# Hybrid encoder block in float32 on one core: own PSUM banks for three products, other pauses in two normalisations, first loads of the second MLP matrix on ScalarE's queue

## The chip, the core and the metric

The program runs on one core of a Trainium2 chip. The metric is the device time of one execution in microseconds (us). Five engines take instructions in order, each from a queue of its own: TensorE (PE), VectorE (DVE), ScalarE (ACT), GpSimd (POOL) and SyncE (SP, which here only issues DMAs). Matrix products are accumulated in PSUM. The kernel uses its eight banks as two rings of four tiles each, called `mm` and `aux`.

## The reference, cut

```python
def block(x, c, ...):                        # 1024 prompt rows, and 8 x 16 sample rows
    ...
    h = rms_norm(x, norm_g[0]) * (1 + sc1) + sh1
    m, conv_state, h_fin, v = mixer(h, ...)                    # ends in "@ w_out"
    x = x + g1 * rms_norm(m, norm_g[1])
    h = rms_norm(x, norm_g[2]) * (1 + sc2) + sh2               # second normalisation
    f = jnp.square(jax.nn.relu(h @ w_ff1)) @ w_ff2             # (1152,1024)x(1024,4096), x(4096,1024)
    x = x + g2 * rms_norm(f, norm_g[3])
    return x, conv_state, h_fin.astype(x.dtype), v
```

## The kernel before, in words

The 1152 rows are 9 tiles of 128, in three groups of three: groups 0 and 1 are prompt rows, group 2 is two prompt tiles (6, 7) and the sample tile (8). A float32 product is made of three: each operand is split into a rounded high part and the low rest (`split`: a CAST, L236 on ACT or L238 on DVE, then a subtraction on DVE, L239), and PE computes high·high, high·low and low·high. With four blocks of depth 128 one *product* is 12 matmuls of 128x384 (`prod`, L1359 to L1361).

In time the program is: the mixer; its output projection, of which `m_out(2)` for group 2 comes last; the first MLP matrix (`m_f1`); the second (`m_f2`).

**`m_f1`** goes through 26 *units*, each one pair p of 128-column blocks of w_ff1 for one or more groups. For groups 0 and 1 together most pairs use a Strassen-like scheme with seven products instead of eight: A11, S2, S1, S3, A12, A22, S4. S1 to S4 are sums of weight blocks (L1330), the other operands T1 to T4 are sums of normalised inputs (`t_task`). Kinds of unit: "g0", "g1", "g2" (one group, four products, PSUM tiles W1 and W2 of `aux`), "fast" (the seven products), "full" (fast and g2 of the same pair interleaved, 11 products). Before: units 0 to 2 are g0, 3 to 5 g1, 6 to 9 fast (NH = 4), then 7 g2 and 9 full.

A fast unit takes three tiles X, Y, Z of `mm`. X collects A11 and then A12, Y collects S2, S3 and A22, Z collects S1 and S4. DVE reads them in between: after S2 `u2 = p1 + Y` (L1467), after S3 `u3 = p1 + Y; u3 += Z` (L1476, L1477), after A22 `p1 += Y` (L1490), after S4 `u2 += Z` (L1500). PE may write Y or Z again only when the read before is done. ACT squares the ReLU of each result (L1369, L1370), and SP stores it.

The weights' operands are prepared five products ahead (`f1_prep(at + 5)`): ACT casts, DVE subtracts. From these results DVE forms sums for the second matrix (`f_sums`, L1382 to L1385), which SP stores in `fdS`. `w_sums` does the same for pieces wt0 to wt15 of w_ff2 (L1402 to L1406), which SP stores in `td`.

**The second normalisation** of group g is `prep2_task(g)`. Per tile: ACT sums the squares (`prep_stat`, L420, into a scratch tile "junk" of the one-buffer ring `tb`, which `f_sums` uses for fS1 too); DVE scales (L465; L452 for the first tile); then twice a half (`prep_half`): four PE transposes into a tile pt2*th* (t the tile, h the half), scale and shift (`modulate`: on ACT, four L428, for tiles 0 to 7; on DVE, L434 and L435, for tile 8), and the split into h2T. Tile 3 to 5 is group 1, 6 to 8 group 2. Group 1's transposes stand partly in `m_out(2)`, partly behind units 0 to 2; group 2's stand in the fast units; `w_sums` begins when group 2 is done.

**What sets the order.** No scheduler: the program steps its tasks by a virtual clock as it is written out, and the table WAIT holds their pauses in virtual nanoseconds. A longer pause puts the next step further back in every engine's queue. The engines then run these queues in order, and wait for data.

**Between the two matrices.** The last unit (25) calls `f2_open` after its S1 product: four DMAs on SP, ar0 and ar1 (stored results, batches A11 and Ga) and br0, br1 (w_ff2). ACT and DVE split these into as0, as1, bs0 and so on, the first operands of `m_f2`, whose first three PSUM tiles P00, P01, P02 are the next of `mm`.

Of the kernel before, what the change touches and what calls it, by code (L numbers as in the profile page):

```python
# [14 lines left out]
ALU = mybir.AluOpType  # L15
# [3 lines left out]
P = 128  # L19
# [3 lines left out]
GT = 3  # L23
GW = 384
DFF = 4096
NG = 3
NH = 4
GELU_A = 0.044715
GELU_S = 0.7978845608028654

# [11 lines left out]
def shape_constants():  # L42
# [20 lines left out]
    pn0=1900, pn1=0, pn2=3800, prep1_load=17400, prep1_load1=1700, prep1_load2=3200, prep1_next=13800,  # L63
    prep1_next1=4400, prep1_next2=1000, prep1_norm=11500, prep1_norm1=3300, prep1_norm2=800, prep1_split=40000,
    prep1_split1=400, prep1_split2=1000, prep1_stat=6500, prep1_stat1=1000, prep1_stat2=0, prep1_tr=5600,
    prep1_tr1=0, prep1_tr2=3500, prep2_load=1700, prep2_load0=200, prep2_load1=5200, prep2_load2=3600,
    prep2_next=3200, prep2_next0=1500, prep2_next1=4400, prep2_next2=1500, prep2_norm=6200, prep2_norm0=9900,
    prep2_norm1=7200, prep2_norm2=2600, prep2_split=1700, prep2_split0=800, prep2_split1=800, prep2_split2=0,
    prep2_stat=9600, prep2_stat0=0, prep2_stat1=4400, prep2_stat2=1200, rr=11700, rr0=800, rr1=13000, rr2=400,
    set_load=10000, set_pcc=0, set_pw=2900, sp=13000, sp0=800, sp1=500, sp2=1900, sp_mid=22500, sp_mid0=9600,  # L70
    sp_mid1=0, sp_mid2=1400, sz=20900, sz0=1300, sz1=800, sz2=0, x1=14700, x10=7300, x11=7200, x12=4700, xr=29300,
    xr0=10000, xr1=2600, xr2=2700, yT=45700, yT0=2500, yT1=5600, yT2=2800, yc=23700, yc0=15400, yc1=16900,
# [11 lines left out]
def wait(key, g=""):  # L84
    return float(WAIT.get(f"{key}{g}", WAIT[key]))
# [33 lines left out]
def tile_block(ctx, tc, io, out):  # L119
    nc = tc.nc  # L120
    pe, act, dve, pool, sync = nc.tensor, nc.scalar, nc.vector, nc.gpsimd, nc.sync
    load = sync.dma_start
# [29 lines left out]
    def mmt(name):  # L152
        return ps.tile([P, 512], F32, tag="mm", name=name)

    def auxt(name):
        return ps.tile([P, 512], F32, tag="aux", name=name)
# [77 lines left out]
    def split(hi, lo, src, on_act=False):  # L234
        if on_act:
            act.copy(hi, src)  # L236
        else:
            dve.tensor_copy(hi, src)  # L238
        dve.tensor_tensor(lo, src, hi.bitcast(F32), op=ALU.subtract)  # L239
# [7 lines left out]
    def transpose4(src, name):  # L247
        pt = auxt(name)
        for k in range(4):
            pe.transpose(pt[:, P * k:P * k + P], src[:, P * k:P * k + P], ident)  # L250
        return pt
# [99 lines left out]
    modT = {}  # L351
# [71 lines left out]
    def modulate(h, src, t, which, half):  # L423
        G, sh = modT[f"G{which}"], modT[f"sh{which}"]
        if t < 8:
            for k in range(4):
                kk = 4 * half + k
                act.activation(h[:, k, :], src[:, k, :], AF.Identity, scale=G[:, kk, 0:1], bias=sh[:, kk, 0:1])  # L428
        else:
            v = src.rearrange("p k (s i) -> p k s i", s=8)  # L430
            h4 = h.rearrange("p k (s i) -> p k s i", s=8)
            gb = G[:, 4 * half:4 * half + 4, 1:9].unsqueeze(3).to_broadcast([P, 4, 8, 16])
            sb = sh[:, 4 * half:4 * half + 4, 1:9].unsqueeze(3).to_broadcast([P, 4, 8, 16])
            dve.tensor_tensor(h4, v, gb, op=ALU.mult)  # L434
            dve.tensor_tensor(h4, h4, sb, op=ALU.add)  # L435

    def prep_half(x, t, dst, off, half):
        pt = transpose4(x[:, 512 * half:512 * half + 512], f"pt2{t}{half}")
        h = x[:, 512 * half:512 * half + 512].rearrange("p (k i) -> p k i", k=4)
        modulate(h, pt.rearrange("p (k i) -> p k i", k=4), t, 2, half)  # L440
        yield wait("prep2_split", t // GT) if t < 8 else 300.0
        for k0, n, d in dst[half]:
            split(d[:, :, 0, off:off + P], d[:, :, 1, off:off + P], h[:, k0:k0 + n, :], ENG["p2hi"])
# [796 lines left out]
    p1 = laneB.add(prep1_task(2, ssd_tasks[1]))  # L1240
# [14 lines left out]
    TV = {}  # L1255
# [43 lines left out]
    units = [(p, "g0") for p in range(NG)] + [(p, "g1") for p in range(NG)]  # L1299
    units += [(p, "fast") for p in range(NG, NG + NH)] + [(p, "g2") for p in range(NG + NH)]  # L1300
    units += [(p, "full") for p in range(NG + NH, NU)]
    FULL = ("A11", "S2", "S1", "S3", "A12", "A22", "S4", "A21")
# [46 lines left out]
    def two(name):  # L1349
        t = wp.tile([P, 2, GW], F32, tag="raw", name=name, bufs=2)  # L1350
        return t[:, 0], t[:, 1]
# [4 lines left out]
    def prod(bank, op, xs, first, last):  # L1356
        for k in range(4):
            x = xs[k]
            pe.matmul(bank, op[:, 0, k, :], x[:, 0], start=first and k == 0, stop=False, skip_group_check=True)  # L1359
            pe.matmul(bank, op[:, 0, k, :], x[:, 1], start=False, stop=False, skip_group_check=True)  # L1360
            pe.matmul(bank, op[:, 1, k, :], x[:, 0], start=False, stop=last and k == 3, skip_group_check=True)  # L1361
# [4 lines left out]
    def f_out(n, p, src, q=None):  # L1366

        q = src if q is None else q
        act.activation(q, src, AF.Relu)  # L1369
        act.activation(q, q, AF.Square)  # L1370
        if n != "A21":
            f_save(n, p, q)
# [38 lines left out]
    def m_f1():  # L1411
        at = 0
        for u, (p, kind) in enumerate(units):
# [8 lines left out]
            def take(n):  # L1422
                nonlocal at
                at += 1
                f1_prep(at + 5)
                return ops[u, n]
# [29 lines left out]
            X, Y, Z = [mmt(f"{n}{u}")[:, 0:GW] for n in "XYZ"]  # L1456
            o = take("A11")
            prod(X, o, hk(0, 0), True, True)
            pu = ta.tile([P, 2, GW], F32, tag="x", name=f"pu{u}", bufs=2)
            p1, u2 = pu[:, 0], pu[:, 1]  # L1460
# [10 lines left out]
            if u == len(units) - 1:  # L1471
                f2_open()
            yield 12 * 175.0
            prod(Y, take("S3"), TV[3], False, True)
            u3, a11 = two(f"u3_{u}")
            dve.tensor_tensor(u3, p1, Y, op=ALU.add)  # L1476
            dve.tensor_tensor(u3, u3, Z, op=ALU.add)  # L1477
            f_out("A22", p, u3)
            yield 12 * 175.0
            o = take("A12")  # L1480
# [5 lines left out]
                f_out("Ga", p, W1, qa)  # L1486
            yield 12 * 175.0
            o = take("A22")
            prod(Y, o, TV[4], False, True)
            dve.tensor_tensor(p1, p1, Y, op=ALU.add)  # L1490
            f_out("A12", p, p1)
            if full:
# [26 lines left out]
    ops2, araw, asp, braw = {}, {}, {}, {}  # L1519
    pos2 = dict(job=0, araw=0, braw=0)  # L1520

    def a_load(upto):
        while pos2["araw"] <= min(upto, len(batches) - 1):
            k = pos2["araw"]
            i, q, n = batches[k]
            if k % 4 == 1:
                araw[k] = fp.tile([P, 4, GW], F32, tag="t2", name=f"ar{k}")
            else:
                araw[k] = fslot((2, None, 0, 1)[k % 4], [P, 4, GW], F32, f"ar{k}")
            load(out=araw[k], in_=fd[n][q])  # L1530
            pos2["araw"] += 1

    def b_load(upto):
        while pos2["braw"] <= min(upto, len(jobs2) // 2 - 1):
            r = pos2["braw"]
            i, u = jobs2[2 * r]
            b = PASSES[i][1]
            t = fp.tile([P, KD, P], F32, tag="raw1", name=f"br{r}", bufs=4).rearrange("p (u k) i -> p u (k i)", u=2)
            if b in td:
                finish(ws)  # L1540
                load(out=t, in_=td[b][u // 2])
            else:
                x, c = int(b[1]) - 1, int(b[2]) - 1
                load(out=t, in_=wv[x][:, u:u + 2, 512 * c:512 * c + 512])
            braw[r] = t
            pos2["braw"] += 1

    def f2_open():
        a_load(1)
        b_load(1)  # L1550

    def f2_prep(upto):
        while pos2["job"] < min(upto, len(jobs2)):
# [214 lines left out]
```

## Time and profile before

| | us |
|---|---|
| three executions | 1393.88, 1397.48 (median), 1398.32 |
| the profiled execution, its own time | 1396.9 |
| its span in the profile | 1395.1 |
| busy in the span: PE, DVE, ACT, POOL | 1278.1, 858.7, 609.5, 255.2 |

The span is what the profiler saw between first and last instruction; 1.8 us of the execution lie outside it. PE is busy 92% of the span, but the engines' shares are averages over stages: in the fast units PE waits, and in the full units it doesn't. "Idle before" in a row is the time in which the engine did nothing before that instruction, and the name behind the arrow is what ended it.

### The profile page before, as it was taken

What the parts mean: (1) busy time and instruction counts of PE and PEld (TensorE: products, weight loads), DVE (VectorE), ACT (ScalarE), POOL (GpSimd) and SP (SyncE); (2) the same over time, 40 slices, a digit from 0 to 9 for tenths busy, and PEclk for the clock granted to TensorE, in tenths of its full rate; (3) what the DMA queues carried; (4) which work ended last, traced back from release to release, by engine and by line L of the source; (5) the groups of instructions that cost most, each with busy time, mean ns of one, the idle gap of its engine ahead of it and who ended that gap; (6) DMA issues with size and microseconds to landing.
All of it is one profiled execution on the core that took longest, in us unless ns stands there. A gap on an engine that the chain in (4) does not pass through costs nothing.

```text
span 1395.1 us, 18656 instructions
## 1 busy us (share of the span) xinstructions
PE 1278.1 (92%) x6815; PEld 1132.2 (81%) x6815; DVE 858.7 (62%) x1349; ACT 609.5 (44%) x1131; POOL 255.2 (18%) x275
## 2 busy tenths in 40 slices
PE   6988888898989999789789999999799999999996
PEld 4966867687789967679689999999788888887874
DVE  4667799466676633687675566766553335336766
ACT  3333423344445524765535444444443334344461
POOL 1233574136341443220000000000000000001013
PEclk9999889999999999889999999999999999999998
DMA  8687646735687558656258865656694437345863
GB/s 312 206 283 260 204 143 207 256 136 187 200 314 251 191 204 318 234 176 217 87 175 300 311 235 199 241 213 213 222 369 154 157 134 267 144 155 185 316 242 120
DMA packets 106259, 304.70 MB, mean 218 GB/s; under 512 B 11844, under 2 KB 32324, under 8 KB 106168
## 3 DMA queue, kind: packets, MB, share of 16 engines
q1 hardware_dynamic: 106056, 303.21, 62.0%
q8 instruction: 53, 0.87, 0.3%
q14 instruction: 38, 0.31, 0.1%
q0 software_dynamic: 112, 0.31, 0.1%
HBM read 231.43 MB, written 72.04 MB: 218 GB/s over the span
## 4 chain that ended last, share of the span: by engine, by line
PE 62%; DVE 14%; DMA 11%; ACT 6%; issue 4%; POOL 2%; SPq 1%; DVEq 0%; ACTq 0%; POOLq 0%
PE P L1630 4%; PE P L1631 4%; PE P L1629 4%; PE W L1360 4%; PE W L1361 4%; PE W L1359 4%; PE G L1630 3%; PE G L1629 3%; PE G L1631 3%; DMA kl<-wl 2%; DMA wr<-in_w_a_dram 2%; PE Y L1359 2%; PE Y L1361 1%; PE Y L1360 1%; DMA x<-in_x_prompt_dram 1%
## 5 line engine op out<-in xcount | busy, mean ns | idle before, releaser
L239 DVE TENSOR_TENSOR bs<-br,bs 128x512 fp32r<-128x512 f32 x128 | 93.7, 748 | 124.1 <-ACT bs L236 124.0
L236 ACT CAST bs<-br 128x512 fp32r<-128x512 f32 x128 | 77.7, 618 | 163.7 <-PE G L1631 102.9
L1630 PE MATMUL P<-bs,as 128*128 128x512 f32 x336 | 132.7, 395 | 3.0 <-DVE bs L239 3.0
L1629 PE MATMUL P<-bs,as 128*128 128x512 f32 x336 | 132.8, 395 | 1.0 <-DVE acc L1692 1.0
L1631 PE MATMUL P<-bs,as 128*128 128x512 f32 x336 | 132.6, 395 | 0.0
L243 POOL TENSOR_SCALAR fr<-fss 128x1 f32<-128x1 f32 x9 | 2.8, 316 | 635.0 <-DVE fss L1589 634.9
L239 DVE TENSOR_TENSOR as<-ar,as 128x1536 fp32r<-128x1536 f32 x44 | 81.0, 1845 | 57.9 <-ACT as L236 57.9
L327 POOL TENSOR_TENSOR wl<-wr,wh 128x1024 fp32r<-128x1024 f32 (+1 forms) x28 | 70.0, 2503 | 110.0 <-ACT wh L320 50.1
L236 ACT CAST as<-ar 128x1536 fp32r<-128x1536 f32 x44 | 64.9, 1479 | 48.1 <-PE P L1631 28.3
L1630 PEld LDWEIGHTS P<-bs,as 128*128 128x128 f32 x336 | 63.4, 189 | 18.1 <-DVE bs L239 3.9
L1629 PEld LDWEIGHTS P<-bs,as 128*128 128x128 f32 x336 | 63.5, 189 | 16.5 <-DVE acc L1692 1.9
L315 ACT CAST wh<-wr 128x1024 fp32r<-128x1024 f32 (+1 forms) x44 | 46.1, 1048 | 69.7 <-PE wo L1000 23.0
L1630 PE MATMUL G<-bs,as 128*128 128x512 f32 x192 | 75.4, 393 | 0.0
L1631 PEld LDWEIGHTS P<-bs,as 128*128 128x128 f32 x336 | 63.5, 189 | 14.5
L1629 PE MATMUL G<-bs,as 128*128 128x512 f32 x192 | 75.2, 392 | 0.0
L1631 PE MATMUL G<-bs,as 128*128 128x512 f32 x192 | 75.2, 392 | 0.0
L596 PE MATMUL xbc<-hT,wl 128*128 128x384 f32 x144 | 51.3, 356 | 4.3 <-DMA wl<-kl 4.3
L643 DVE SCALAR_TENSOR_TENSOR cva<-pre,cwh,cva 128x256 f32<-128x256 f32 (+1 forms) x78 | 44.5, 611 | 13.9 <-ACT pre L624 12.1
L594 PE MATMUL xbc<-hT,wh 128*128 128x384 f32 x144 | 52.2, 362 | 0.0
L595 PE MATMUL xbc<-hT,wh 128*128 128x384 f32 x144 | 50.6, 351 | 0.0
L583 PE MATMUL pv<-wh,hT 128*128 128x256 f32 x144 | 43.1, 300 | 3.3 <-DVE vt L566 3.3
L584 PE MATMUL pv<-wl,hT 128*128 128x256 f32 x144 | 41.8, 290 | 4.0 <-POOL wl L327 4.0
(945 smaller groups left out, 3782.3 us busy)
## 6 DMA issues: line engine op xcount, KB each, us to landing
wf<-in_w_f_dram SPq DMA_DIRECT2D x52, 512.0 KB, 5.4
wl<-kl SPq DMA_DIRECT2D x42, 512.0 KB, 4.3
wt<-in_w_ff_dram SPq DMA_DIRECT2D x16, 1024.0 KB, 6.0
td<-wt SPq DMA_DIRECT2D x64, 256.0 KB, 2.6
br<-in_w_ff_dram SPq DMA_DIRECT2D x32, 512.0 KB, 3.9
br<-td SPq DMA_DIRECT2D x32, 512.0 KB, 3.6
kl<-wl SPq DMA_DIRECT2D x26, 512.0 KB, 6.6
wr<-in_w_o_dram SPq DMA_DIRECT2D x24, 512.0 KB, 5.3
```

The source lines that it names most:

```text
L236: act.copy(hi, src)
L239: dve.tensor_tensor(lo, src, hi.bitcast(F32), op=ALU.subtract)
L327: (pool if i in LO_POOL else dve).tensor_tensor(lo, raw, hi.bitcast(F32), op=ALU.subtract)
L594: pe.matmul(out, wh, xh, start=first, stop=False)
L595: pe.matmul(out, wh, xl, start=False, stop=False)
L596: pe.matmul(out, wl, xh, start=False, stop=last)
L1359: pe.matmul(bank, op[:, 0, k, :], x[:, 0], start=first and k == 0, stop=False, skip_group_check=True)
L1360: pe.matmul(bank, op[:, 0, k, :], x[:, 1], start=False, stop=False, skip_group_check=True)
L1361: pe.matmul(bank, op[:, 1, k, :], x[:, 0], start=False, stop=last and k == 3, skip_group_check=True)
L1629: pe.matmul(bank, x[:, 0], b[:, 0], start=first, stop=False, skip_group_check=True)
L1630: pe.matmul(bank, x[:, 0], b[:, 1], start=False, stop=False, skip_group_check=True)
L1631: pe.matmul(bank, x[:, 1], b[:, 0], start=False, stop=last, skip_group_check=True)
```

## The change

Five edits:

1. NH is 5: one pair moves from a full unit to a fast and a g2 unit. There are now 27 units: 3 g0, 3 g1, 5 fast (6 to 10), 8 g2, 8 full. The products are the same in number.
2. In fast and full units S3 has a tile Y7 of its own (`mm`) and A22 a tile Y4 (`aux`): Y, Y7 and Y4 are each written once. `p1 = u2 + Y7; u3 = p1 + Z` replaces the two additions after S3. X and Z are still written twice.
3. Group 1's pauses are shorter, group 2's longer.
4. For second halves of tiles 3, 4, 5 scale and shift are four operations on DVE (new L442) in place of four on ACT.
5. `f2_open` issues its four DMAs on ScalarE's queue.

```diff
-NH = 4
+NH = 5
...
-    prep1_tr1=0, prep1_tr2=3500, prep2_load=1700, prep2_load0=200, prep2_load1=5200, prep2_load2=3600,
-    prep2_next=3200, prep2_next0=1500, prep2_next1=4400, prep2_next2=1500, prep2_norm=6200, prep2_norm0=9900,
-    prep2_norm1=7200, prep2_norm2=2600, prep2_split=1700, prep2_split0=800, prep2_split1=800, prep2_split2=0,
-    prep2_stat=9600, prep2_stat0=0, prep2_stat1=4400, prep2_stat2=1200, rr=11700, rr0=800, rr1=13000, rr2=400,
+    prep1_tr1=0, prep1_tr2=3500, prep2_load=1700, prep2_load0=200, prep2_load1=1500, prep2_load2=3600,
+    prep2_next=3200, prep2_next0=1500, prep2_next1=2500, prep2_next2=5000, prep2_norm=6200, prep2_norm0=9900,
+    prep2_norm1=3500, prep2_norm2=5000, prep2_split=1700, prep2_split0=800, prep2_split1=800, prep2_split2=1500,
+    prep2_stat=9600, prep2_stat0=0, prep2_stat1=2500, prep2_stat2=4500, rr=11700, rr0=800, rr1=13000, rr2=400,
...
-        modulate(h, pt.rearrange("p (k i) -> p k i", k=4), t, 2, half)
+        if half and t // GT == 1:
+            for k in range(4, 8):
+                dve.tensor_scalar(h[:, k - 4, :], pt[:, P * (k - 4):P * (k - 3)], modT["G2"][:, k, 0:1],
+                                  modT["sh2"][:, k, 0:1], op0=ALU.mult, op1=ALU.add)
+        else:
+            modulate(h, pt.rearrange("p (k i) -> p k i", k=4), t, 2, half)
...
-            prod(Y, take("S3"), TV[3], False, True)
+            Y = mmt(f"Y7{u}")[:, 0:GW]
+            prod(Y, take("S3"), TV[3], True, True)
             u3, a11 = two(f"u3_{u}")
-            dve.tensor_tensor(u3, p1, Y, op=ALU.add)
-            dve.tensor_tensor(u3, u3, Z, op=ALU.add)
+            dve.tensor_tensor(p1, u2, Y, op=ALU.add)
+            dve.tensor_tensor(u3, p1, Z, op=ALU.add)
             f_out("A22", p, u3)
...
-            prod(Y, o, TV[4], False, True)
+            Y = auxt(f"Y4{u}")[:, 0:GW]
+            prod(Y, o, TV[4], True, True)
             dve.tensor_tensor(p1, p1, Y, op=ALU.add)
...
-    def a_load(upto):
+    def a_load(upto, load=load):
...
-    def b_load(upto):
+    def b_load(upto, load=load):
...
     def f2_open():
-        a_load(1)
-        b_load(1)
+        a_load(1, act.dma_start)
+        b_load(1, act.dma_start)
```

How this moves instructions is shown at three places (the first matmul of a group stands for it; names carry the tile and the unit).

**PE, end of `m_out(2)` and the first units.** pt2*th* are transposes, wo21x matmuls of `m_out(2)`, W10 and W20 the first unit's products. Before:

```order
L250 MATMUL pt231_5347<-cs_81,M1_4566 128x128 x4
...
L250 MATMUL pt220_5368<-cs_81,A0_4956 128x128 x4
...
L250 MATMUL pt221_5414<-cs_81,A0_4956 128x128 x4
L250 MATMUL pt240_5425<-cs_81,M1_4566 128x128 x4
L1359 MATMUL W10_5434<-h2T00_5055,op0A11_5388 128x384
...
L250 MATMUL pt241_5555<-cs_81,M1_4566 128x128 x4
...
L250 MATMUL pt250_5655<-cs_81,M1_4566 128x128 x4
...
L250 MATMUL pt251_5750<-cs_81,M1_4566 128x128 x4
L1359 MATMUL W13_5779<-h2T100_5052,op3A11_5632 128x384
```

Now:

```order
L250 MATMUL pt240_5299<-cs_81,M1_4566 128x128 x4
...
L250 MATMUL pt211_5343<-cs_81,A0_4956 128x128 x4
...
L250 MATMUL pt241_5358<-cs_81,M1_4566 128x128 x4
...
L250 MATMUL pt220_5399<-cs_81,A0_4956 128x128 x4
...
L250 MATMUL pt250_5417<-cs_81,M1_4566 128x128 x4
L250 MATMUL pt221_5458<-cs_81,A0_4956 128x128 x4
L250 MATMUL pt251_5469<-cs_81,M1_4566 128x128 x4
L1364 MATMUL W10_5478<-h2T00_5055,op0A11_5428 128x384
```

All of group 1's transposes now stand ahead of the first unit; three of them stood behind units 0, 1 and 2.

**PE, fast unit 7.** T20, T1, T3, T4 and h2T are the input sides of its products; M2 is group 2. Before:

```order
L1359 MATMUL X7_6212<-h2T00_5055,op7A11_6091 128x384
L250 MATMUL pt261_6232<-cs_81,M2_5026 128x128 x4
L1359 MATMUL Y7_6213<-T20_5454,op7S2_6116 128x384
L1359 MATMUL Z7_6214<-T1_5453,op7S1_6138 128x384
L250 MATMUL pt270_6294<-cs_81,M2_5026 128x128 x4
L1359 MATMUL Y7_6213<-T3_5456,op7S3_6158 128x384
L1359 MATMUL X7_6212<-h2T01_5056,op7A12_6186 128x384
L250 MATMUL pt271_6354<-cs_81,M2_5026 128x128 x4
L1359 MATMUL Y7_6213<-T4_5457,op7A22_6215 128x384
L1359 MATMUL Z7_6214<-h2T11_5054,op7S4_6243 128x384
```

Now (Y77 and Y47 are unit 7's new tiles Y7 and Y4):

```order
L1364 MATMUL X7_6197<-h2T00_5055,op7A11_6091 128x384
L1364 MATMUL Y7_6198<-T20_5498,op7S2_6117 128x384
L250 MATMUL pt260_6239<-cs_81,M2_5026 128x128 x4
L1364 MATMUL Z7_6199<-T1_5497,op7S1_6138 128x384
L1364 MATMUL Y77_6282<-T3_5500,op7S3_6158 128x384
L1364 MATMUL X7_6197<-h2T01_5056,op7A12_6179 128x384
L1364 MATMUL Y47_6331<-T4_5501,op7A22_6200 128x384
L250 MATMUL pt261_6348<-cs_81,M2_5026 128x128 x4
L1364 MATMUL Z7_6199<-h2T11_5054,op7S4_6219 128x384
```

Two halves of group 2 stand in this unit where three stood; pt270 to pt281 now stand in units 8 to 10.

**SP before, ACT now, around `f2_open`.** SP before:

```order
L1408 DMA td47_5024<-wt14_8984 128x512
L1364 DMA fdS13_4972<-fS1_14_9115 128x384
L1364 DMA fdS23_4976<-fS2_14_9116 128x384
L1364 DMA fdS33_4980<-pu24_8858 128x384
L1364 DMA fdS43_4984<-fS4_14_9117 128x384
L1530 DMA ar0_9141<-fdA110_4957 128x1536
L1530 DMA ar1_9143<-fdGa0_4985 128x1536
L1544 DMA br0_9145<-in_w_ff2_dram 128x2x512
L1544 DMA br1_9147<-in_w_ff2_dram 128x2x512
```

ACT now:

```order
L236 CAST op26S4_9116<-S4_26_9114 128x512
L236 CAST op26A21_9145<-wf261_8708 128x512
L1537 DMA ar0_9160<-fdA110_4957 128x1536
L1537 DMA ar1_9162<-fdGa0_4985 128x1536
L1551 DMA br0_9164<-in_w_ff2_dram 128x2x512
L1551 DMA br1_9166<-in_w_ff2_dram 128x2x512
L236 CAST as0_9169<-ar0_9160 128x4x384
L236 CAST as1_9172<-ar1_9162 128x4x384
...
L1374 ACTIVATE u3_26_9190<-u3_26_9190 128x384
```

The four loads stood behind eight stores on SP; now they stand behind a cast on ACT.

## Rows read from the trace of the kernel before

**Rows 1.** The view of windows: stretches of `m_f1` and the change of matrix. After the window and its length: busy us and, in brackets, instructions of PE, PE's weight loads, DVE, ACT, POOL; then PE's granted clock (1.00 is 2.4 GHz, 0.50 is 1.2 GHz), the DMA share and GB/s.
```profile
600.00:640.00 40.00, 33.01 (x179) 32.07 (x178) 35.94 (x59) 25.02 (x56) 2.88 (x2) 0.91 0.56 167
...
651.00:736.00 85.00, 68.69 (x363) 66.67 (x362) 56.95 (x104) 40.60 (x83) 2.23 (x6) 0.92 0.41 139
...
736.00:990.00 254.00, 254.00 (x1455) 254.00 (x1455) 161.76 (x268) 121.71 (x233) 0.00 (x0) 1.00 0.69 242
...
990.00:1013.00 23.00, 15.37 (x78) 14.81 (x77) 9.73 (x13) 10.97 (x18) 0.00 (x0) 0.85 0.75 249
```

**Rows 2.** PE's timeline from the end of `m_out(2)` to unit 3: instructions that PE was idle before. Columns: start, duration, engine, line, operation, tiles, shapes, count, and in brackets the idle time and what ended it.
```profile
567.54 0.63 PE L250 MATMUL pt<-cs,A 128*128 128x128 f32 x4 [3.04 <-DVE A L465]
...
583.83 0.44 PE L1359 MATMUL W<-h2T,op0A 128*128 128x384 f32 x1 [1.46 <-ACT op0A L236]
...
590.65 0.46 PE L1360 MATMUL W<-h2T,op0A 128*128 128x384 f32 x1 [2.07 <-DVE h2T L239]
...
622.44 0.66 PE L1359 MATMUL W<-h2T,op3A 128*128 128x384 f32 x1 [5.70 <-DVE h2T L238]
...
627.59 0.41 PE L1359 MATMUL W<-h2T,op3A 128*128 128x384 f32 x1 [1.07 <-DVE h2T L238]
```

**Rows 3.** DVE's timeline of the same stretch, two rows.
```profile
575.93 0.43 DVE L238 CAST h2T<-A 128x512 fp32r<-128x512 f32 x1 [5.03 <-ACT A L428]
...
587.87 2.73 DVE L239 TENSOR_TENSOR h2T<-A,h2T 128x512 fp32r<-128x512 f32 x1
```

**Rows 4.** PE's timeline in the fast units: the instructions that PE was idle before, and the last matmul of unit 9.
```profile
664.09 0.44 PE L1359 MATMUL Y<-T,op6A 128*128 128x384 f32 x1 [2.21 <-DVE u L1476]
...
681.83 1.11 PE L250 MATMUL pt<-cs,M 128*128 128x128 f32 x4 [6.09 <-DVE M L465]
...
696.88 0.66 PE L250 MATMUL pt<-cs,M 128*128 128x128 f32 x4 [2.92 <-DVE M L465]
...
712.40 0.44 PE L1359 MATMUL Y<-T,op8A 128*128 128x384 f32 x1 [2.38 <-DVE u L1476]
...
725.48 0.66 PE L1359 MATMUL Y<-T,op9S 128*128 128x384 f32 x1 [2.31 <-DVE pu L1467]
...
731.71 0.45 PE L1359 MATMUL Y<-T,op9A 128*128 128x384 f32 x1 [0.38 <-DVE u L1476]
...
735.84 0.34 PE L1361 MATMUL Z<-h2T,op9S 128*128 128x384 f32 x1
```

**Rows 5.** DVE's timeline: the first read of Y in unit 6, and a stretch from the reads of unit 8 to those of unit 9.
```profile
655.69 0.56 DVE L1467 TENSOR_TENSOR pu<-pu,Y 128x384 f32<-128x384 f32 x1
...
712.38 0.55 DVE L1477 TENSOR_TENSOR u<-u,Z 128x384 f32<-128x384 f32 x1
...
714.59 0.69 DVE L239 TENSOR_TENSOR op9S<-S,op9S 128x512 fp32r<-128x512 f32 x1 [1.66 <-ACT op9S L236]
...
719.38 0.69 DVE L239 TENSOR_TENSOR op9A<-wf,op9A 128x512 fp32r<-128x512 f32 x1 [1.66 <-ACT op9A L236]
...
724.18 0.69 DVE L239 TENSOR_TENSOR op9S<-S,op9S 128x512 fp32r<-128x512 f32 x1 [0.68 <-ACT op9S L236]
...
724.78 0.55 DVE L1467 TENSOR_TENSOR pu<-pu,Y 128x384 f32<-128x384 f32 x1
...
731.69 0.55 DVE L1477 TENSOR_TENSOR u<-u,Z 128x384 f32<-128x384 f32 x1
```

**Rows 6.** ACT's timeline in the fast units: two waits for group 2's normalisation, and two of the stretch of the group before.
```profile
661.19 1.06 ACT L420 ACTIVATE junk<-M 128x1024 bf16<-128x1024 f32 x1 [4.96 <-DMA fdS<-fS]
...
682.98 1.51 ACT L428 ACTIVATE M<-pt,mod_sh,mod_G 128x128 f32<-128x128 f32 x4 [3.87 <-PE pt L250]
...
712.96 0.53 ACT L1369 ACTIVATE u<-u 128x384 f32<-128x384 f32 x1 [1.81 <-DVE u L1477]
...
717.76 0.53 ACT L1369 ACTIVATE pu<-pu 128x384 f32<-128x384 f32 x1 [1.22 <-DVE pu L1490]
```

**Rows 7.** SP's timeline at `f2_open`: its DMA issues (duration is the time on SP's queue).
```profile
983.08 4.93 SPq L1408 DMA_DIRECT2D td<-wt  x4
...
988.15 1.79 SPq L1364 DMA_DIRECT2D fdS<-fS  x2
...
991.03 0.39 SPq L1530 DMA_DIRECT2D ar<-fdA  x1
```

**Rows 8.** ACT's timeline there: the last cast of `m_f1`, the first of `m_f2`.
```profile
985.77 0.62 ACT L236 CAST op25A<-wf 128x512 fp32r<-128x512 f32 x1 [0.69 <-PE Y L1361]
...
995.35 1.47 ACT L236 CAST as<-ar 128x1536 fp32r<-128x1536 f32 x1 [8.96 <-DMA ar<-fdA]
```

**Rows 9.** DVE's timeline there.
```profile
996.86 1.76 DVE L239 TENSOR_TENSOR as<-ar,as 128x1536 fp32r<-128x1536 f32 x1 [6.60 <-ACT as L236]
...
1001.77 0.55 DVE L1477 TENSOR_TENSOR u<-u,Z 128x384 f32<-128x384 f32 x1
...
1009.86 0.55 DVE L1500 TENSOR_TENSOR pu<-pu,Z 128x384 f32<-128x384 f32 x1
```

**Rows 10.** PE's timeline there: the last matmul of the A12 product of group 2, and the first of A22.
```profile
993.82 0.34 PE L1361 MATMUL W<-h2T,op25A 128*128 128x384 f32 x1
...
1001.79 0.69 PE L1359 MATMUL Y<-T,op25A 128*128 128x384 f32 x1 [7.63 <-DVE u L1476]
```

**Rows 11.** The view of DMA, 940 to 1060 us: issues by tensor, KB each, and the median us from issue to landing.
```profile
br<-in_w_ff_dram SPq DMA_DIRECT2D x12, 512.0 KB, 8.9
...
ar<-fdA SPq DMA_DIRECT2D x6, 768.0 KB, 6.6
```

## The prediction

> **What bounds the kernel now.** I read the windows by stage first [rows 1]: after 736 us PE issues 1455 matmuls in 254.00 us without an idle moment, 2.1 us a product. In the fast units (651 to 736) it is busy 68.69 of 85.00 us at a granted clock of 0.92, and at the change of matrix 15.37 of 23.00 us at 0.85. So the change can win only ahead of 736 and around 1000 us, and whatever it moves between the units behind 736 costs nothing while that stretch stays full. Then I read who ends PE's waits. In `m_out(2)` and the first units it is the scaled or split input [rows 2]. In the fast units it is DVE's read of Y ("DVE u L1476") and the scaled rows of group 2 ("DVE M L465") [rows 4]. At 1001.79 it is again the read of Y, after 7.63 us [rows 10].
>
> The second question is what DVE waits for before those reads. From unit 8 to unit 9 DVE waits only for ACT, and ACT only for DVE [rows 5, 6]. A result goes from DVE to ACT (712.38 to 712.96), there ReLU, square and the cast of the next operand follow in order, and the cast lets DVE go on (714.59, after 1.66 us idle), whose next sum lets ACT go on (717.76, after 1.22 us). This runs from u3 of unit 8 (712.38) to the first read of unit 9 (724.78) in 12.4 us, and from there to u3 of unit 9 (731.69) in 6.9 us, in which four operations of `w_sums` and one split stand in place of two weight sums and one trip to ACT; that nearly cancels (I take 0.5 off). A fast unit therefore costs this chain 18.8 us, and PE 7 x 2.1 = 14.7 us. PE's wait for Y is a symptom: the bank comes late because the chain is late.
>
> **Group 1 earlier, its second halves on DVE.** Gone are the waits of unit 3, 5.70 + 1.07 us [rows 2], with some 1.6 us of lower clock behind them (0.91 in that window [rows 1]). But three halves more, with 12 operations that are new on DVE (and gone from ACT), now fall into `m_out(2)`, where PE already waits 3.04, 1.46 and 2.07 us for DVE and ACT [rows 2]. Their price on DVE: three splits of about 1.1 us (0.43 for the cast [rows 3], 0.69 for the subtraction [rows 5]), two scalings of 0.75, and eight of the new operations. No row shows one of these; it lies between 0.37 (a quarter of ACT's 1.51 [rows 6]) and 0.55 (a DVE operation of 384 columns [rows 5], these have 128), and I take 0.4, nearer to the row for the same piece. That is 3.3 + 1.5 + 3.2 = 8.0 us, and one more split that takes 2.73 us where its neighbours take 0.69 [rows 3] makes it 10. DVE's idle 5.03 us there [rows 3] covers half, so PE loses about 5 us against 8.4 gained, and comes to the fast units about 3.4 us earlier. The chain doesn't: from 600 to 640 us DVE is busy 35.94 of 40 us [rows 1], and the work is the same. I put unit 6's first read at 655.0 in place of 655.69 [rows 5]; bounds 652 and 658.
>
> The Trainium skill's "Perfetto Trace Analysis", section Matmuls, says that independent groups should rotate through different PSUM banks, so that the reading of one overlaps the next group's matmuls; by that the fast units would run at PE's pace, which is the first rival below. The ACT-DVE rows speak against it here.
>
> **Own banks and the fifth fast unit.** S3 and A22 no longer wait for a read. S4 still does: Z is read in u3 and written again by S4, two products later. DVE's operations stay equal in number. So the chain sets the pace, five times. Before, from unit 6's first read to u3 of unit 9 it was 731.69 - 655.69 = 76.0 us, of which 3 x 18.8 + 6.9 = 63.3 are the bare chain and 12.7 are group 2's normalisation in it, with waits such as ACT's 4.96 us for the buffer of the sum of squares and 3.87 us for transposes [rows 6]. The same pieces now lie over units 6 to 10: I take 11.5 (about 2 of those waits go, 0.9 comes, because two of the sums of squares now stand ahead of a cast that DVE waits for). Then u3 of unit 10 ends at 655.0 + 4 x 18.8 + 7.0 + 11.5 = 748.7, S4 follows, and the next unit starts at 748.7 + 0.4 + 2.1 = 751.2. Before, the same products would be done at 736.0 (the last matmul of unit 9 is at 735.84 [rows 4]) + 14.7 = 750.7. Cost 0.5 us; bounds: 20 gained (the chain is no limit) and 11 lost (below). Behind that PE has all it needs, and the three extra splits and 1 MB of weights of the extra unit lie beside full PE work. `w_sums` begins a unit or two later, and its last pieces move into the first pass of `m_f2`; they are needed only when later passes load them, so I cost that at nothing; without that cover it is a few operations of 0.7 us on DVE.
>
> **The loads on ScalarE's queue.** On SP, ar0 is issued at 991.03, because four stores of `td` waited 4.93 us from 983.08 for DVE, and four of `fdS` follow [rows 7]. On ACT the place is behind the last cast, 985.77 + 0.6 [rows 8]; the tiles that ar0 and ar1 overwrite are read last by the S2 product, for whose end that cast waits. So they issue at 986.3, 4.7 us earlier. The first split of as0 on DVE, 996.86, and u3, 1001.77 [rows 9], come 4.7 us earlier too: u3 is done at 997.6. A22 no longer waits: PE goes on at 994.0 [rows 10] through A22 and its second use (4.2 us), and needs Z for S4 at 998.2. The wait of 7.63 us is gone, and with it some 1.4 us of low clock (0.85 [rows 1]), together 9.0. What is late next: the third bank of the second matrix is Z's buffer. It is free after u2's read (L1500, 1009.86 [rows 9], just after S4's end), which stands on DVE behind the splits of bs1 to bs3 and a piece of `w_sums`. 4.7 us earlier that is 1005.2, plus 0.6 for itself, where PE wants the bank at about 1003.6: 2.2 us, and up to 1.7 us of clock. I take a gain of 6.0 us; bounds 2 (the transfers land no sooner, third rival) and 9.
>
> The rule of the Trainium skill's "DMA: Bandwidth & Descriptors", section Issuing engines are not separate DMA queues, is that issuing on several engines saves only the issue time on the sequencer. By it the loads would gain no more than such slots, which is the third rival below. In the rows it isn't the slots but the order on SP that holds ar0: 4.93 us of waiting for DVE.
>
> **Sum.** 0.5 - 6.0 = -5.5 on the profiled execution's 1396.9 (span 1395.1, 1.8 outside): 1391.4. That execution is 0.6 below the median of the three runs, 1397.48, so against the runs it would be 1392.0. I say 1392.0. A measurement of this kernel tells about 0.3%, 4.2 us, from no change, so this is just a visible gain (limit 1393.3).
>
> **Rivals.**
> First, the banks free PE, because the chain was stretched by PE's waits and not the other way. For it: PE's waits name reads of Y five times [rows 4, 10]. Against it: between 712 and 725 neither DVE nor ACT waits for PE [rows 5, 6]. In full: from 651 PE would need 5 x 14.7 + 2 = 75.5 and start the next unit at 726.5 in place of 750.7, 24 earlier: 1368. Half of it is 1380. Chance 0.13.
> Second, slower: the ring closes. ACT's scale-and-shift of a half stands in order ahead of casts. If its transposes stand on PE behind a product that waits for the chain, the chain waits for itself. Before this cost ACT 3.87 us once [rows 6]. Now pt271 stands behind S4 of unit 8, pt280 behind S3 of unit 9 and pt281 behind unit 10's A11, so it can happen three times: 11.6 us, time 1392.0 + 11.6 = 1403.6. It decides when ACT waits for such a transpose by more than about 1 us each time. Chance 0.20.
> Third, the loads land no sooner, since `td`, `fdS` and the pending transfers share the DMA engines with them: ar takes 6.6 us and br 8.9 us in that stretch already [rows 11]. Then only the issue slots of eight stores are saved, 8 x 0.39 = 3.1 us [rows 7], of which about 1 goes to the third bank: a gain of 2, so 1396. The change would then not do what it says: a wait on Y replaced by one on Z. Chance 0.20.
>
> **Chances and range.** My forecast has 0.42, and the rest, 0.05, is unnamed, mostly group 1's work costing more in `m_out(2)`. Faster by over 0.3% (below 1393.3): 0.13 + 0.31 of the forecast + 0.03 = 0.47. Slower (above 1401.7): 0.15 of the second rival + 0.04 = 0.19. Within: 0.34. The likeliest case by itself spans 1386 to 1397. The range takes in half of the first rival and most of the second, 1380 to 1403.
>
> **What would show it.** Right: first reads of fast units some 19 to 21 us apart, with DVE and ACT waiting for each other; PE's waits there named after u3 or Z and not Y; ar issued near 986 at the corresponding place, no wait at A22, a wait of about 2 us at the third matmul group of the second matrix; no wait of 5.70 at unit 3 and new ones of 1 to 4 us in `m_out(2)` and unit 0. Wrong: fast units 15 to 16 us apart (first rival), ACT waiting several times for transposes (second), ar landing at its old distance from A22 (third).

## The result and the profile after

Six executions of the changed kernel took 1382.12 to 1387.33 us, median 1384.45; six of the kernel before, in turn with them, 1393.34. The ratio is 0.994 (95% interval 0.9918 to 0.9962): 5 to 11 us faster. A second series gave 0.9956 (0.9939 to 0.9972). The forecast was 5.5 us, 0.39%, and 1392.0 against the three runs known then, whose median was 4.1 us above that of the six. So 1384.45 lies inside the stated range, 1380 to 1403, but below the 1386 to 1397 of the likeliest case.

The profiled execution took 1387.33 us, its span is 1385.6. Its windows answer to [rows 1]: the fast units, the full stretch, three pieces of the change of matrix (columns as there).

```profile
643.00:746.00 103.00, 83.87 (x444) 81.72 (x443) 70.03 (x127) 49.70 (x101) 2.23 (x6) 0.93 0.37 126
746.00:980.00 234.00, 234.00 (x1336) 234.00 (x1335) 146.10 (x238) 114.38 (x219) 0.00 (x0) 1.00 0.69 246
980.00:985.00 5.00, 5.00 (x31) 5.00 (x30) 3.81 (x7) 0.94 (x2) 0.00 (x0) 1.00 0.68 213
985.00:990.00 5.00, 5.00 (x31) 5.00 (x30) 0.00 (x0) 0.17 (x1) 0.00 (x0) 1.00 1.03 383
990.00:1005.00 15.00, 12.10 (x58) 11.43 (x57) 9.27 (x12) 8.85 (x14) 0.00 (x0) 0.89 0.47 173
```

The full stretch is as full as before. PE still waits in the fast units, and at the change of matrix it is busy up to 990 and beyond. PE's longer waits, from its timeline (answering to [rows 2], [rows 4] and [rows 10]):

```profile
580.26 0.51 PE L1364 MATMUL W<-h2T,op0A 128*128 128x384 f32 x1 [1.86 <-ACT op0A L236]
...
587.70 0.69 PE L1364 MATMUL W<-h2T,op0A 128*128 128x384 f32 x1 [3.37 <-DVE h2T L238]
...
615.70 0.45 PE L1366 MATMUL W<-h2T,op3A 128*128 128x384 f32 x1 [1.04 <-DVE op3A L239]
...
657.88 0.41 PE L1364 MATMUL Z<-h2T,op6S 128*128 128x384 f32 x1 [2.64 <-DVE u L1483]
...
677.86 0.41 PE L1364 MATMUL Z<-h2T,op7S 128*128 128x384 f32 x1 [2.57 <-DVE u L1483]
...
688.77 0.66 PE L250 MATMUL pt<-cs,M 128*128 128x128 f32 x4 [2.25 <-DVE M L470]
...
712.56 0.66 PE L250 MATMUL pt<-cs,M 128*128 128x128 f32 x4 [3.12 <-DVE M L470]
...
741.88 0.66 PE L1364 MATMUL Z<-h2T,op10S 128*128 128x384 f32 x1 [5.01 <-DVE u L1483]
...
997.25 0.66 PE L1364 MATMUL Z<-h2T,op26S 128*128 128x384 f32 x1 [2.90 <-DVE u L1483]
```

The waits for Y are gone; in their place PE waits for Z before every S4, and at the change of matrix 2.90 us there in place of 7.63 at A22. The 5.70 of unit 3 is gone, unit 0 waits longer (1.86 and 3.37 us). DVE's first reads in units 6 to 10 come 18.9, 21.6, 23.2 and 21.2 us apart; 19 to 21 was the sign of being right, 15 to 16 that of being wrong. In the fast units DVE still waits for ACT alone (its timeline in unit 8, answering to [rows 5]):

```profile
697.56 0.56 DVE L1483 TENSOR_TENSOR u<-pu,Z 128x384 f32<-128x384 f32 x1
...
700.82 0.69 DVE L239 TENSOR_TENSOR op9S<-S,op9S 128x512 fp32r<-128x512 f32 x1 [1.64 <-ACT op9S L236]
...
705.62 0.69 DVE L239 TENSOR_TENSOR op9A<-wf,op9A 128x512 fp32r<-128x512 f32 x1 [1.66 <-ACT op9A L236]
...
709.82 0.69 DVE L239 TENSOR_TENSOR op9A<-wf,op9A 128x512 fp32r<-128x512 f32 x1 [3.05 <-ACT op9A L236]
...
714.40 0.55 DVE L1472 TENSOR_TENSOR pu<-pu,Y 128x384 f32<-128x384 f32 x1
```

The longest, 3.05 us, is the cast behind a scale-and-shift in ACT's order (its timeline):

```profile
706.80 0.53 ACT L1374 ACTIVATE pu<-pu 128x384 f32<-128x384 f32 x1 [1.22 <-DVE pu L1507]
707.36 0.53 ACT L1375 ACTIVATE pu<-pu 128x384 f32<-128x384 f32 x1
707.79 1.49 ACT L428 ACTIVATE M<-pt,mod_sh,mod_G 128x128 f32<-128x128 f32 x4
709.16 0.62 ACT L236 CAST op9A<-wf 128x512 fp32r<-128x512 f32 x1
```

No fast unit shows ACT waiting for transposes. The table compares two profiled executions of each kernel (the second ones are `before_again` and `after_again`), us. "Start" is the first matmul of group 2's output projection; nothing differs ahead of it. "Next unit" is the first unit behind the fast ones; in the changed kernel it is set 14.7 us earlier than measured, since a fifth fast unit's products are done by then. This takes 14.7 us off the row that ends there and adds them to the row that starts there.

| | before | changed |
|---|---|---|
| start in the span (scatter of the mixer) | 538.2, 535.4 | 532.5, 534.4 |
| start to X of unit 6 | 113.1, 112.5 | 110.0, 108.9 |
| start to first read of unit 6 | 117.5, 116.9 | 118.2, 117.0 |
| from there to the next unit | 80.3, 79.3 | 80.5, 78.9 |
| next unit to the second matrix | 275.7, 277.0 | 271.8, 271.3 |
| from there to the end of the span | 383.4, 382.0 | 382.7, 383.4 |

So the gain that the profiles show, 4.2 us by the means of the pairs, lies between the next unit and the second matrix, 4.8, less 0.6 elsewhere. The full stretch is without idle time in both kernels, so the 4.8 are the change of matrix. The rest of the measured 6 to 8 us is not placed: the start scatters by more than that, and only two profiles of the kernel before exist.

### The profile page after: what moved, and what is told of

Its sections match the earlier page's. It is cut to its first block, busy times and chain, and to the rows that moved or that the text cites. A ratio compares the mean times of both kernels' runs of the same rounds, so it can differ in the third digit from the quotient of the medians.

```text
span 1385.6 us, 18661 instructions
## 1 busy us (share of the span) xinstructions
PE 1275.2 (92%) x6815; PEld 1131.3 (82%) x6815; DVE 863.4 (62%) x1364; ACT 605.9 (44%) x1122; POOL 256.6 (19%) x275
## 4 chain that ended last, share of the span: by engine, by line
PE 43%; DVE 8%; ACT 2%; issue 2%; DMA 1%; POOL 0%; SPq 0%; DVEq 0%; ACTq 0%; POOLq 0%
PE P L1637 5%; PE P L1638 5%; PE P L1636 5%; PE G L1637 3%; PE G L1636 3%; PE G L1638 3%; PE W L1366 3%; PE W L1365 3%; PE W L1364 3%; PE Y L1364 1%; PE Y L1366 1%; PE Y L1365 1%; PE Z L1364 1%; PE Z L1366 1%; PE Z L1365 1%
## 5 line engine op out<-in xcount | busy, mean ns | idle before, releaser
L588 PE MATMUL pz<-wh,hT 128*128 128x264 f32 (+1 forms) x144 | 43.1, 299 | 3.6 <-DVE sz L711 1.9
```

Source lines behind the costliest of these rows:

```text
L588: pe.matmul(o, xs[:, k, 0], wh[:, k, :], start=first, stop=False)
```

## The experiments

All times are medians; the ratio is to the kernel before in the same series.

**The loads back on SP** (`sp_open`).

```diff
-        a_load(1, act.dma_start)
-        b_load(1, act.dma_start)
+        a_load(1)
+        b_load(1)
```

> The changed kernel with the four first loads of the second matrix back on SP's queue, all else as changed. My theory (order on SP holds ar0 back): ar0 issued about 4.7 us later against the S3 product of the last unit, S4 waits for u3 some 5 us longer than in the changed kernel, total +4 to +6 us, about 1389 to 1390. Rival (transfers land no sooner from ScalarE's queue): +2 us or less, S4's wait about the same.

1390.25 us, ratio 0.9973 (0.995 to 0.9996): 2.4 to 4.6 us slower than the changed kernel by its two ratios, whose intervals overlap this one, and 3.0 to 5.8 by its two medians; my theory had 4 to 6, the rival 2 at most. SP's issue of ar0, ACT's last cast ahead of it and PE's wait before S4 in `sp_open`:

```profile
986.86 1.08 SPq L1537 DMA_DIRECT2D ar<-fdA  x1
...
983.70 0.62 ACT L236 CAST op26A<-wf 128x512 fp32r<-128x512 f32 x1 [1.49 <-PE Y L1366]
...
1001.45 0.66 PE L1364 MATMUL Z<-h2T,op26S 128*128 128x384 f32 x1 [5.21 <-DVE u L1483]
```

So with the other edits in place the order on SP holds ar0 3.2 us behind the start of the last cast, where it was 5.3 in the kernel before (991.03 against 985.77): the 4.93 us of `td` in [rows 7] aren't there. S4 waits 5.21 us, 2.3 more than 2.90 (2.1 more than the 3.08 of `after_again`). In the wait the queue is worth half of the 4.7 us that I had; the times are too close to tell more.

**Four fast units** (`nh4`).

```diff
-NH = 5
+NH = 4
```

> The changed kernel with four fast units again (NH = 4), all else as changed. My theory: a fast unit costs the ACT-DVE chain 18.8 us where PE needs 14.7 for its products, so the fifth one costs 4.1 us: 1380 to 1381, next unit after the fast ones about 4 us earlier for the same number of products. Rival (own banks free PE, so a fast unit costs no more than its products): no change, 1384 within 1.5.

1380.33 us, ratio 0.9908 (0.9878 to 0.9939): 4.1 us below the changed kernel's 1384.45 (4.5 to 6.7 by the ratios). So the fifth fast unit costs more than its products, as the chain theory has it. In the profile the next unit starts 72.8 us behind the first read of unit 6, in place of 80.5 and 78.9 for the same products: 6 to 8 us earlier, where I had about 4. Then it waits 2.49 us for group 2's h2T, which gives a part back.

**A tile of its own for S4** (`own_z`).

```diff
             dve.tensor_tensor(u3, p1, Z, op=ALU.add)
+            dve.tensor_tensor(u2, u2, Z, op=ALU.add)
...
-            prod(Z, take("S4"), hk(1, 1), False, True)
+            Z = auxt(f"Z4{u}")[:, 0:GW]
+            prod(Z, take("S4"), hk(1, 1), True, True)
```

> The changed kernel with a tile of its own for S4 as well; DVE then does one more addition of 0.55 us in each fast or full unit. Theory chain (ACT and DVE wait for each other, 19 to 23 us a fast unit): PE's waits before S4 (2.64, 2.57, 1.01, 2.54, 5.01 us, 13.8 in all) move to another place and the time changes by -1 to +3 us; first reads of fast units stay 19 to 23 us apart. Theory bank (PE waits for a PSUM bank, and the rest follows from that): the 13.8 us are won, about 1371.

1385.0 us, ratio 0.9942 (0.9922 to 0.9962): the time of the changed kernel. This separates the theories: PE no longer waits for any read before S3, A22 or S4, and DVE's first reads of units 6 to 10 stand as far apart as they stood (`own_z`'s DVE timeline):

```profile
650.13 0.55 DVE L1472 TENSOR_TENSOR pu<-pu,Y 128x384 f32<-128x384 f32 x1
...
668.95 0.55 DVE L1472 TENSOR_TENSOR pu<-pu,Y 128x384 f32<-128x384 f32 x1
...
691.11 0.55 DVE L1472 TENSOR_TENSOR pu<-pu,Y 128x384 f32<-128x384 f32 x1
...
714.30 0.55 DVE L1472 TENSOR_TENSOR pu<-pu,Y 128x384 f32<-128x384 f32 x1
...
735.55 0.55 DVE L1472 TENSOR_TENSOR pu<-pu,Y 128x384 f32<-128x384 f32 x1
```

85.4 us in all, against 85.0 (650.66 to 735.61) in the changed kernel. PE's waits moved (its timeline):

```profile
688.68 1.11 PE L250 MATMUL pt<-cs,M 128*128 128x128 f32 x4 [6.61 <-DVE M L470]
...
712.46 0.66 PE L250 MATMUL pt<-cs,M 128*128 128x128 f32 x4 [4.00 <-DVE M L470]
...
732.03 0.44 PE L1364 MATMUL X<-h2T,op10A 128*128 128x384 f32 x1 [2.25 <-ACT pu L1466]
...
996.60 0.50 PE L1638 MATMUL G<-bs,as 128*128 128x512 f32 x1 [0.99 <-DVE pu L1498]
...
999.42 0.50 PE L1638 MATMUL G<-bs,as 128*128 128x512 f32 x1 [1.86 <-DVE pu L1509]
```

In its one profile PE does leave the fast units earlier, 88.3 us behind the first read of unit 6 in place of 95.2 and 93.6, since S4 of the last fast unit no longer waits. The second matrix then takes 377.0 us from its first matmul to PE's last in place of 370.8 and 371.5. Two of G's three tiles there have the buffers of Y4 and Z4, and behind the two waits for these the granted clock is 0.83 from 1000 to 1010 us. That `own_z` ends at no gain is measured; that these 5.5 to 6.2 us are why rests on one profile.

**ReLU and square on DVE in fast units** (`relu_dve`), for u3, p1 and u2 (`on_dve=not full`).

```diff
+        if on_dve:
+            dve.scalar_tensor_tensor(q, src, 0.0, src, op0=ALU.max, op1=ALU.mult)
+        else:
             act.activation(q, src, AF.Relu)
             act.activation(q, q, AF.Square)
```

> The changed kernel with ReLU and square of three results of each fast unit (u3, p1, u2) in one DVE operation each in place of two on ACT, same values. Theory chain: three trips from DVE to ACT and back leave the chain, at some 1.8, 1.2 and 1.2 us of waiting plus 1 us of ACT work each, DVE gets 3 x 0.55 more; first reads of fast units come 15 to 17 us apart in place of 19 to 23, and the time falls by 15 to 25 us, about 1360 to 1369. Theory bank: S4 still waits for u3, DVE has more to do, and the time stays or rises by up to 8 us.

1373.16 us, ratio 0.9847 (0.9815 to 0.988): 0.9 to 1.1% below the changed kernel's ratios, 13 to 15 us; the bank theory is out. First reads are 16.0, 18.7, 18.4 and 19.1 us apart, mostly above the 15 to 17 that I gave. DVE seems to be the next limit: it is busy 63.31 of 73 us from the first such read to the last (the window of this kernel, columns as in [rows 1]), and `best2` below tests that:

```profile
653.00:726.00 73.00, 67.34 (x373) 66.26 (x373) 63.31 (x115) 31.26 (x65) 2.66 (x6) 0.95 0.41 141
```

The same four intervals in the changed kernel, with DVE busy 56.65 of 85 us:

```profile
651.00:736.00 85.00, 70.88 (x381) 69.02 (x380) 56.65 (x102) 42.63 (x87) 2.23 (x6) 0.94 0.34 119
```

**Both kernels once more** (`before_again`, `after_again`).

> The kernel before once more, for a second profile of it. If the 5.7 us by which group 2's output projection begins earlier in the changed kernel's profile than in that of before (523.7 against 529.4 us; nothing is changed ahead of it) are scatter of the mixer, this profile shows another time there, within 3 us of the changed kernel's ones; if they belong to the changed program, it shows 529 again. From there to the end of the span: 863 to 868 us, as in the first profile (865.7).

> The changed kernel once more, for a second profile and for its time beside the next two on the same chip. Scatter: output projection of group 2 begins anywhere from 523 to 530 us; from there to the end 859 to 864 us; ratio to before 0.992 to 0.997.

`before_again` took 1392.39 us (one execution) and starts group 2's projection 2.8 us earlier than the first profile of the same program: scatter. The 529.4 and 523.7 of the expectations are where the last quarter of group 1's projection begins, 8.8 us ahead of the start in the table (538.2 and 532.5); the difference of 5.7 is the same. From the table's start to the end the two kernels took 855.2 and 850.6 us, which is 864.0 and 859.4 as I counted there, inside both expectations. `after_again`: 1387.21, ratio 0.9956 (0.9939 to 0.9972). The starts of all kernels here lie between 531.4 and 538.2, so 5.7 us between two profiles proves nothing.

**u3 ahead of the first splits** (`u3_first`).

```diff
-                f1_prep(at + 5)
+                f1_prep(min(at + 5, len(jobs)) if n == "S3" else at + 5)
```

> The changed kernel with one step later: the split of the first operands of the second matrix is written behind the sums u3 of the last unit, so DVE reads Z as soon as S3 is done and not behind as0, as1 and bs0. My theory (DVE's order holds Z back until ar has landed): the 2.9 us before S4 go, and the low clock behind them, 3 to 4.5 us faster than the changed kernel, about 1380; the second matrix starts when S4 and A21 are done. Rival (the landing of ar and br bounds the change of matrix): the wait moves to the first matmul of the second matrix, gain under 1 us.

1382.57 us, ratio 0.9929 (0.9906 to 0.9952), 4.6 us less than `after_again` in the same series (1.5 to 3.8 less by the changed kernel's two ratios; the intervals overlap). PE has no wait from the last unit into the second matrix, whose first matmul comes 465.6 us after the start, against 470.5 and 467.2. DVE's timeline shows the step:

```profile
986.35 0.55 DVE L1483 TENSOR_TENSOR u<-pu,Z 128x384 f32<-128x384 f32 x1
991.14 1.76 DVE L239 TENSOR_TENSOR as<-ar,as 128x1536 fp32r<-128x1536 f32 x1 [4.23 <-ACT as L236]
```

So Z was ready 10 us before DVE came to read it in the changed kernel (996.55, with the same start, 532.5): the read stood in order behind the splits of loads that had not landed.

**Own banks alone** (`banks_only`): the kernel before with the two hunks on Y7 and Y4.

> The kernel before with the own tiles for S3 and A22 alone (four fast units, pauses, ACT's scale and shift, loads on SP as before). My theory: in the fast units the ACT-DVE chain keeps its pace, first reads of units 6 to 9 some 69 us apart in all as before (724.8 - 655.7), within 3 us, and PE's waits are named after u3 before S4; at the change of matrix A22 no longer waits and S4 waits 3.5 to 5 us in place of 7.6 to 8.0. Together 3 to 6 us faster than before, about 1388 to 1391. Rival (banks free PE in the fast units): 10 us or more faster than before, 1384 or less.

1390.12 us, ratio 0.9971 (0.9952 to 0.9989): 1.5 to 6.7 us faster than before, as expected. The first reads of units 6 to 9 span 67.9 us (650.68 to 718.57), against 69.1 and 68.0 before. The wait at the change of matrix is 3.77 us at S4 (PE's timeline of `banks_only`):

```profile
996.75 0.41 PE L1359 MATMUL Z<-h2T,op25S 128*128 128x384 f32 x1 [3.77 <-DVE u L1478]
```

From the next unit to the second matrix it takes 272.4 us, against 275.7 and 277.0 before and 271.8 and 271.3 changed. So by its profile the own banks alone, with the loads still on SP, bring most of the gain at the change of matrix.

**Group 1 as before** (`old_g1`): its four pauses as before, scale and shift on ACT.

> The changed kernel with group 1's pauses and scale and shift on ACT as before. My theory: the wait of 5 to 6 us at unit 3 is back and the 3 to 5 us in unit 0 go; the fast units start 2 to 4 us later, their first read, set by the chain, at most 1.5 us later; the time is within 2 us of the changed kernel's. Rival (group 1 earlier is where the rest of the gain comes from): 4 us or more slower than the changed kernel.

1390.9 us (1381.91 to 1397.88), ratio 0.9968 (0.9946 to 0.9989): 1.7 to 3.9 us slower than the changed kernel by the ratios. This lies between the two expectations and its interval overlaps the changed kernel's: inconclusive. In the profile the first read of unit 6 comes 117.5 us after the start (118.2 and 117.0 in the changed kernel), as I expected. What I had not expected: the first reads of units 6 to 10 span 87.5 us, where the changed kernel has 85.0 and 85.2. The 2 us stand between units 6 and 7 (21.0 against 18.9). There ACT waits for the store that frees the buffer of "junk" (ACT's timeline of `old_g1`):

```profile
661.28 1.06 ACT L420 ACTIVATE junk<-M 128x1024 bf16<-128x1024 f32 x1 [5.12 <-DMA fdS<-fS]
```

In the changed kernel it waits less there (its timeline):

```profile
654.30 1.06 ACT L420 ACTIVATE junk<-M 128x1024 bf16<-128x1024 f32 x1 [3.76 <-DVE op7A L239]
```

So by this one profile group 1's earlier place is worth some 2 us of the chain in unit 6.

**Group 2's pauses as before** (`old_p4`).

> The changed kernel with group 2's pauses as before, so that its transposes stand in units 6 to 8 again and the stores and sums for the second matrix start earlier. My theory: the pieces cost the chain the same wherever they stand in the fast units, so the sum over the fast units stays within 2 us and the time within 2 us of the changed kernel's. Rival (spreading the pieces is worth something, since PE's waits of 6.1 and 2.9 to 3.4 us for scaled rows of group 2 come back): 4 to 6 us slower.

1388.11 us, ratio 0.9959 (0.9941 to 0.9978): 0.4 to 2.6 us slower than the changed kernel by the ratios, well inside the intervals. My sum over the fast units failed, though: first reads span 88.7 us, not 85.0. In the profile the loss comes back at the change of matrix, where S4 waits 0.74 us and not 2.90. The queues suggest the reason: here the 1 MB load of `w_sums` is issued 4.3 us ahead of ar0, and ar0's cast follows 4.6 us after the issue. SP's timeline of `old_p4`:

```profile
979.44 0.38 SPq L1404 DMA_DIRECT2D wt<-in_w_ff_dram  x1
```

ACT's timeline of it, issue and cast:

```profile
983.78 0.36 ACTq L1537 DMA_DIRECT2D ar<-fdA  x1
...
988.35 1.49 ACT L236 CAST as<-ar 128x1536 fp32r<-128x1536 f32 x1 [3.95 <-DMA ar<-fdA]
```

In the changed kernel that load is issued 0.5 us ahead of ar0. SP's timeline of it:

```profile
981.28 0.38 SPq L1404 DMA_DIRECT2D wt<-in_w_ff_dram  x1
```

And there the cast follows the issue after 8.0 us (ACT's timeline):

```profile
981.81 0.37 ACTq L1537 DMA_DIRECT2D ar<-fdA  x1
...
989.83 1.48 ACT L236 CAST as<-ar 128x1536 fp32r<-128x1536 f32 x1 [7.40 <-DMA ar<-fdA]
```

That the load ahead is the cause is argued from these two profiles. In `sp_open` ar0 takes 7.6 us from issue to cast though the load stands 3.7 us ahead of it; there four stores of `fdS` are issued in between.

**A faster version** (`best1`, then `best2`). `best1` is the changed kernel with the edits of `relu_dve`, `nh4` and `u3_first`; `best2` also casts group 2's high parts on ACT:

```diff
-            split(d[:, :, 0, off:off + P], d[:, :, 1, off:off + P], h[:, k0:k0 + n, :], ENG["p2hi"])
+            split(d[:, :, 0, off:off + P], d[:, :, 1, off:off + P], h[:, k0:k0 + n, :], ENG["p2hi"] or t >= 2 * GT)
```

> Three edits on top of the changed kernel: ReLU and square of u3, p1, u2 in fast units on DVE, four fast units in place of five, u3 of the last unit ahead of the first splits of the second matrix. If they add up: 11.3 (measured) + 3.6 (a fast unit is then 18.3 us by DVE's busy time, against 14.7 of PE) + 3.5 = 18 us less than the changed kernel, about 1366. If the four fast units are too few for the pieces of group 2 (the next unit waits for its h2T): 1370.

> The faster version of before this (ReLU and square of three results on DVE in fast units, four fast units, u3 ahead of the first splits of the second matrix) with the high parts of group 2's normalised rows cast on ACT and not on DVE: nine casts of 0.29 to 0.43 us leave DVE, 3.1 us. If DVE's busy time sets the fast units: 2 to 3 us faster, about 1368. If the trips to ACT come back with it: no change or 2 us slower.

`best1`: 1370.31 us, ratio 0.9836 (0.9811 to 0.9862), 16.9 us below `after_again` in its series where I had 18: the edits nearly add up. But the time is also the 1370 that I gave for four fast units being too few, and the sign of that is there (PE's timeline of `best1`):

```profile
718.53 0.62 PE L1364 MATMUL W<-h2T,op10A 128*128 128x384 f32 x1 [2.73 <-DVE h2T L238]
```

`best2`: 1366.02, ratio 0.9801 (0.9785 to 0.9817), 1.8 to 2.2% faster than the kernel before. Its first reads are 16.1, 17.6 and 17.2 us apart, in `best1` 16.1, 18.7 and 18.4: 2.2 us less over the three intervals, for 3.1 us of casts taken off DVE. This is what I expected if DVE's busy time sets the fast units then. The two times are 4.3 us apart, in different series, and the intervals of the ratios just overlap.

## Why the prediction was right, point by point

**The chain sets the pace of the fast units: right.** I put the five fast units, first read of unit 6 to the next unit, at 751.2 - 655.0 = 96.2 us; the profiles show 95.2 and 93.6. Against before I had +0.5 for everything up to the next unit; by the table's first profiles and by its second ones it is +0.9 and -0.2. `own_z`, `banks_only` and `relu_dve` show that the banks don't decide it and the trips to ACT do. So PE's waits changed their name from Y to Z, as forecast. The parts fit less well than their sum: the fifth unit cost 4.1 to 6.7 us by the times of `nh4` where I had 18.8 - 14.7 = 4.1, and I had put the gain from spreading group 2 at 1.2 us (12.7 to 11.5), where `old_p4` shows 3.7.

The Trainium skill's "Perfetto Trace Analysis", section Matmuls, has independent groups rotate through different PSUM banks, so that one group's reading overlaps the next one's matmuls. In the fast units the rows and `own_z` speak against a gain by it: the reader was late with banks of their own too. At the change of matrix it did gain, since A22's own tile lets PE run two products further.

**Group 1 earlier: right, with one gain not foreseen.** PE comes to unit 6 some 3.3 us earlier after the start (forecast 3.4), the first read does not (+0.4; forecast -0.7, within its bounds). The four new DVE operations take 0.40 us each, as bounded. I had the chain unchanged behind that read; `old_g1` shows some 2 us gained in unit 6, in one profile.

**The change of matrix: right in sum, partly by luck; two terms were mis-sized.** I had 9.0 gained less 2.2 for the third bank and part of the clock, 6.0; the profiles show 4.8. The loads do issue 5.3 us earlier, counted from the start of ACT's last cast: ar0 issues together with it, at 981.81, and before it issued 5.3 us behind it (991.03 against 985.77). That as0 and u3 come 4.7 us earlier too failed: as0's cast starts 8.0 us behind that last cast in place of 9.6, 1.6 us gained, since ar0 needed 8.0 us from issue to cast where it had needed 4.3. The busy share of the DMA engines reads 1.03 there, from 985 to 990, with the load of `w_sums` issued 0.5 us before ar0. So the third rival held in part: `sp_open` gives 2.3 us of wait for the queue, between the rival's 2 and my 4.7, and `banks_only` gets most of the stage's gain without it.

The Trainium skill's "DMA: Bandwidth & Descriptors", section Issuing engines are not separate DMA queues, has all of them run on the same 16 DMA engines. The trace fits it: of the 5.3 us by which the loads issue earlier, 1.6 are left at as0's cast.

"The third bank of the second matrix is Z's buffer" failed the other way (PE's timeline of the changed kernel, then DVE's):

```profile
1004.34 0.40 PE L1636 MATMUL P<-bs,as 128*128 128x512 f32 x1
...
1004.62 0.55 DVE L1507 TENSOR_TENSOR pu<-pu,Z 128x384 f32<-128x384 f32 x1
```

PE starts P02 without a wait, before DVE's read of Z. By the addresses in the two programs P02 has the buffer of X now and had that of Y before; Z's comes back only in the second pass, in both. So I had read the ring wrongly. A wait of 2.9 at S4 that I had at zero, and one of 2.2 at P02 that isn't there, nearly cancel: that the sum came out this close is luck.

**The rivals.** Banks free PE: out for the pace of the fast units (`own_z`, `banks_only`); only the way out of the last one gets shorter. The closed ring: out, ACT never waits for a transpose there; the pieces cost in order, 3.05 us at 709.82, but the sum is no more than before. Spreading group 2 is worth 3.7 us in the fast units by `old_p4`, given back at the change of matrix.

**What each edit is worth.** Against the changed kernel's two ratios, the loads on ACT bring 2.4 to 4.6 us, group 1 earlier 1.7 to 3.9, group 2 later 0.4 to 2.6, and the fifth fast unit costs 4.5 to 6.7; the own banks alone bring 4.0 against before (interval 1.5 to 6.7). The intervals overlap, so the order of these sizes is not shown. But one of the five edits works against the others: without it the changed kernel takes 1380.33 us.

## What to carry to other kernels

A wait for a PSUM bank names the reader that is late, not the cause: look at what that reader waited for. Where two engines waited for each other, as here, another bank moved the wait and fewer hand-overs shortened it. Before a load is moved to another queue, see what the DMA engines carry at the new time. A read that frees a bank should not stand in order behind work on data that has not landed.

## What was not expected of the hardware

ReLU and square as one DVE operation on 128x384 takes 0.56 us, where ACT takes 0.53 twice, and DVE idles 1.66 us for the cast that stands behind them. With nothing changed ahead of it, group 2's output projection began 531.4 to 538.2 us into the span over all profiles here, and 2.8 us apart in two of the same program: as much as the change is worth.
